# Gated MLP of a two-layer decoder trunk: the fourth chunk pair of each layer by seven half-size block products instead of two plain products, with the three plain pairs left in front of it issued in a new order

## The chip, the cores and the metric

The kernel runs on one core of one Trainium2 chip, as one launch. The metric is the device time of one execution in microseconds (us). The kernel before takes 1432.87 us, the median of three runs (1432.86 to 1433.24).

## The reference, cut to what matters

```python
def conv_ffn(x, norm, w_up, dw_w, dw_b, w_down):      # D_MODEL 1024, D_FF 3072, SEQ 512, float32
    h = rms_norm(x, norm) @ w_up
    g = causal_dwconv(h[..., :D_FF], dw_w, dw_b)      # width 3
    u = h[..., D_FF:]
    return (jax.nn.gelu(g) * u) @ w_down
```

Both layers end with this block, after a mixer and a cross-attention; the change is in this block alone. Tokens lie along the free axis of every tile (512 of them), channels on the 128 partitions.

## The kernel before

**Precision.** TensorE multiplies `float32r` operands. Each float32 operand is kept as a high part (a copy by ScalarE, ACT) and a low part (the rest, by VectorE, DVE), and each product is three matmuls: high by high, high by low, low by high (`mm3`, L184 to L187). So every weight that is loaded costs a high on ACT and a low on DVE before TensorE (PE) can use it.

**Chunks.** `w_up` has 24 gate chunks and 24 value chunks of 128 columns; gate chunk c and value chunk c make pair c. In each layer `opening` computes pairs 0 to 3 plainly: `start(i)` is one chunk, eight contraction tiles by three matmuls of 512 columns, so 24 matmuls a chunk and 48 a pair. Pairs 4 to 23 go through `unit(c)`: gate and value chunk, the two halves of the contraction and the two halves of the tokens make a two by two block product, which is done with seven products of 4 by 3 matmuls of 256 columns, 84 matmuls in all. Their operands are sums: on the token side T1 to T4, made once per layer by `Seven.sums`; on the weight side the blocks a11, a12, a22, s1, s2, s3, s4. A block is `high(name)` on ACT, then `low(name)` on DVE.

**How the weight sums are made.** `Blocks` holds a pair's four quarter blocks: r and z (one load, `load`, L768), a12 and a22 (two loads, `load_second`, L773 and L774). After the low of a11 an accumulating DMA issued by GpSimd (POOL) adds z to r (L803), which makes s3; after the low of a22 one adds a22 to z (L805), which makes s1; after the low of s3 one adds a22 to r (L807), which makes s2; after the low of s2 one adds a12 to r (L811), which makes s4. So s2 of a pair cannot be copied before s3's low is done and a 256 KB transfer has landed.

**A unit's order.** PE does B11 (a11), B21 (a12), T2 (s2), T3 (s3), then in a unit with a down projection one 12-matmul product of 512 columns (`Down.out`, into an `aux` bank), then T1 (s1), B22 (s4), T4 (a22), and a second `Down.out`. DVE and ACT meanwhile make the blocks of the next pair, add the seven results up (L170), and run `gating` of the pair before: scale by r (the norm's reciprocal, 512 wide), taps (two instructions, L857), Gelu on ACT, product (L861), high `ys[c][0]` (L863) and low `ys[c][1]` (L865). The first `Down.out` of group g needs ys of the four pairs 4g to 4g+3, the last of which was begun in the unit before.

**What sets the order.** PE, ACT, DVE and POOL run in the order in which the code of `opening` and `unit` is written (`manual_schedule` over `ORDERED`). The order of the loads on SyncE's queue (SP) is set by the tile framework's scheduler; each waits there for its buffer: a `raw` buffer (three of them) is free when the low of its last holder is done, a `big` buffer (fifteen) when its last reader is done.

**Names.** `first` and `second` are the first two pairs of `pairs`; `gate(i)`, `values(i)`, `close(i)` are the plain pair's gate branch, product and low of ys; `fetch(i)` loads a plain chunk's weights and makes their high, `w[-1].low()` their low; `rest()` is the end of the last plain pair, done inside the first unit.

Of the kernel before, what the change touches and what calls it, by code (L numbers as in the profile page):

```python
# [15 lines left out]
P = 128  # L16
# [8 lines left out]
CF = D_FF // P  # L25
NG = 6
GC = CF // NG
EPS = 1e-6
AHEAD = 100
PAIRED = (0, 4, 1, 5, 2, 6, 3, 7)  # L30
# [30 lines left out]
def trunk(ctx: ExitStack, tc: tile.TileContext, I: dict, out: list):  # L61
# [751 lines left out]
    def ffn(layer, norm, nxt, seven):  # L813
# [23 lines left out]
        downs = {c: Down(*divmod(c - GC, GC)) for c in range(GC, CF + GC)}  # L837

        def high(c, name):
            if c in pairs:  # L840
                pairs[c].high(name)

        def low(c, name):
            if c in pairs:
                pairs[c].low(name)

        def gating(c, f, g, ps, u3):
# [19 lines left out]
        def unit(c):  # L867
# [19 lines left out]
            ps = m(seven.B21, "a12")  # L887
# [5 lines left out]
            ps = m(seven.T2, "s2")  # L893
# [6 lines left out]
            ps = m(seven.T3, "s3")  # L900
# [11 lines left out]
            if c + 1 in downs:  # L912
# [25 lines left out]
        def opening():  # L938


            nonlocal left, due
            norm.r, ps, y = None, {}, [None] * GC

            def start(i):

                ps[i] = main_ps()
                x = w.pop(0)
                for k in range(C):
                    mm3(ps[i], blk(x, k * P), norm.x[k], k == 0, k == C - 1)

            def fetch(i):
                w.append(Piece(I["wup"][(layer * 2 + i % 2) * GC + i // 2]))
                w[-1].high()

            def gate(c):
# [15 lines left out]
            def values(c):  # L971
                V.tensor_tensor(y[c], ps.pop(2 * c + 1), y[c], op=ALU.mult)
                ys[c] = act_r(), act_r()
                A.activation(ys[c][0], y[c], AF.Copy)

            def close(c):
                V.tensor_tensor(ys[c][1], y[c], ys[c][0].bitcast(F32), op=ALU.subtract)
# [22 lines left out]
            next(g, None)  # L1000

# [36 lines left out]
            pairs[second].load()  # L1038
            pairs[second].load_second()
            downs[first].load()  # L1040
            values(2)
            close(2)
            high(second, "a11")

            start(7)
            downs[first].w.high()
            g = gate(3)
            next(g)
            low(second, "a11")
            next(g)  # L1050
            downs[first].w.low()
            next(g)
            downs[second].load()
            pairs[second + 1].load()
            next(g, None)

            def rest():
                values(3)
                yield
                close(3)  # L1060

            left, due = rest(), None

        left, due = None, None
        first, second = GC, GC + 1
        with tc.high_priority(AHEAD):
            w = [Piece(I["wup"][(layer * 2 + k) * GC]) for k in range(2)]
            for x in w:
                x.high()
                x.low()  # L1070
# [707 lines left out]
def _fours(g, v):  # L1778

    return np.concatenate([g[:, :, :T], v[:, :, :T], v[:, :, T:], g[:, :, T:]], axis=2)  # L1780


def _layout(inputs):
# [5 lines left out]
    for name, width in _PARAMS:  # L1789
# [25 lines left out]
        "wup": np.concatenate([_cols(w[:, at : at + GC * P]) for w in up for at in (0, CF * P)]),  # L1815
        "wpair": np.concatenate([_fours(w[GC:CF], w[CF + GC :]) for w in map(_cols, up)]),
# [22 lines left out]
```

## Time and profile before

| | |
|---|---|
| median of three runs | 1432.87 us |
| profiled execution, its own time | 1434.17 us |
| its span (first to last instruction) | 1432.3 us |
| PE busy | 1419.6 us, 99% of the span |
| DVE busy | 1176.7 us, 82% |
| ACT busy | 798.2 us, 56% |
| POOL busy | 304.4 us, 21% |
| granted TensorE clock | 0.999 |
| the MLP of layer 0 | from about 356 to 716 us of the span |
| the MLP of layer 1 | from about 1044 us on |

The profile is that of one execution, so a sum made from its rows is set against its own 1434.17 us, 1.3 us above the median. The busy share of an engine is an average over stages. PE's matmuls are pipelined: a row's duration is longer than the distance to the next start, and it is the distance that fills the time. In a timeline row the first number is the start in us from the span's start, the second the duration, and what stands in square brackets is the idle time of the engine before the row and what ended it.

### The profile page before, as it was taken

How to read it: one execution, taken by the hardware profiler on the slowest of the kernel's cores; microseconds unless marked ns; L12 is line 12 of the kernel's file. 1: busy time of each engine (PE TensorE's matmuls, PEld its weight loads, DVE VectorE, ACT ScalarE, POOL GpSimd, SP SyncE). 2: the span in 40 equal slices, each digit the busy share in tenths (PEclk: the TensorE clock that was granted, in tenths of full speed). 3: DMA queues.
4: the chain of work that ended last, by engine and by line, in shares of the span. 5: the costliest groups of instructions: out<-in, count | busy, mean ns of one | idle time of the engine just before them, and what ended most of it. 6: DMA issues, size and time to landing. Idle time of an engine off the chain costs nothing.

```text
span 1432.3 us, 22644 instructions
## 1 busy us (share of the span) xinstructions
PE 1419.6 (99%) x8504; PEld 1257.3 (88%) x8504; DVE 1176.7 (82%) x1955; ACT 798.2 (56%) x1321; POOL 304.4 (21%) x317
## 2 busy tenths in 40 slices
PE   9999999999999999999999999999999999999997
PEld 7888888998899999999988777899889999999997
DVE  6987776778788888888888997978778888888885
ACT  7678754666544444544565547767655444444434
POOL 0001310200021221222008992010001222222201
PEclk9999999999999999999999999999999999999999
DMA  8523232542557777777432464345244876787741
GB/s 292 198 81 99 93 118 81 118 111 89 158 136 169 162 182 165 163 173 173 136 123 89 118 167 143 107 87 147 87 129 121 178 179 157 171 184 159 162 126 59
DMA packets 77517, 200.11 MB, mean 140 GB/s; under 512 B 8672, under 2 KB 9952, under 8 KB 77408
## 3 DMA queue, kind: packets, MB, share of 16 engines
q1 hardware_dynamic: 50624, 150.15, 33.6%
q0 software_dynamic: 26496, 48.25, 20.5%
q8 instruction: 67, 1.10, 0.3%
q14 instruction: 42, 0.34, 0.1%
q10 hardware_dynamic: 288, 0.27, 0.1%
HBM read 145.16 MB, written 2.10 MB: 103 GB/s over the span
## 4 chain that ended last, share of the span: by engine, by line
PE 91%; DVE 3%; POOL 2%; DMA 2%; ACT 1%; issue 1%; SPq 0%; POOLq 0%; ACTq 0%; DVEq 0%
PE mm L186 22%; PE mm L185 22%; PE mm L187 22%; PE aux L185 7%; PE aux L186 7%; PE aux L187 7%; PE mm L456 2%; DMA raw<-in_wv 1%; DVE wlo L166 1%; POOL actf L1443 1%; PE aux L529 0%; ACT whi L165 0%; POOL act L166 0%; POOL tmp L1264 0%; DMA raw<-in_win 0%
## 5 line engine op out<-in xcount | busy, mean ns | idle before, releaser
L186 PE MATMUL mm<-act,whi 128*128 128x512 f32 (+2 forms) x1093 | 385.1, 352 | 0.6 <-DVE act L180 0.5
L185 PE MATMUL mm<-act,whi 128*128 128x512 f32 (+2 forms) x1093 | 384.6, 353 | 0.1
L187 PE MATMUL mm<-act,wlo 128*128 128x512 f32 (+2 forms) x1093 | 384.6, 352 | 0.0
L186 PEld LDWEIGHTS mm<-act,whi 128*128 128x128 f32 x1093 | 206.6, 189 | 30.3 <-DVE act L166 1.0
L185 PEld LDWEIGHTS mm<-act,whi 128*128 128x128 f32 x1093 | 206.4, 189 | 30.0 <-ACT tmp L1442 0.8
L187 PEld LDWEIGHTS mm<-act,wlo 128*128 128x128 f32 x1093 | 206.6, 189 | 27.0
L793 ACT ACTIVATE bigr<-raw 128x512 fp32r<-128x512 f32 x160 | 100.7, 630 | 156.7 <-DMA raw<-wa 64.3
L187 PE MATMUL mm<-bigr,bigr 128*128 128x256 f32 x640 | 181.1, 283 | 0.0
L186 PE MATMUL mm<-bigr,bigr 128*128 128x256 f32 x640 | 181.1, 283 | 0.0
L185 PE MATMUL mm<-bigr,bigr 128*128 128x256 f32 x640 | 180.9, 283 | 0.0
L170 DVE TENSOR_TENSOR tmp<-mm,tmp 128x256 f32<-128x256 f32 x322 | 131.2, 420 | 34.7 <-PE mm L187 28.3
L185 PE MATMUL aux<-act,whi 128*128 128x512 f32 x399 | 156.3, 392 | 0.0
L186 PE MATMUL aux<-act,whi 128*128 128x512 f32 x399 | 156.2, 391 | 0.0
L187 PE MATMUL aux<-act,wlo 128*128 128x512 f32 x399 | 155.2, 389 | 0.0
L165 ACT ACTIVATE whi<-raw 128x1024 fp32r<-128x1024 f32 (+1 forms) x95 | 96.6, 1021 | 85.5 <-PE mm L186 44.5
L800 DVE TENSOR_TENSOR bigr<-raw,bigr 128x512 fp32r<-128x512 f32 x160 | 110.0, 688 | 32.4 <-ACT bigr L793 30.4
L186 PEld LDWEIGHTS mm<-bigr,bigr 128*128 128x128 f32 x640 | 122.7, 192 | 1.6
L185 PEld LDWEIGHTS mm<-bigr,bigr 128*128 128x128 f32 x640 | 122.7, 192 | 1.6
L187 PEld LDWEIGHTS mm<-bigr,bigr 128*128 128x128 f32 x640 | 122.7, 192 | 0.0
L803 POOL DMA_DIRECT2D raw<-raw x46 | 39.8, 866 | 350.8 <-DVE wlo L800 303.9
L166 DVE TENSOR_TENSOR wlo<-raw,whi 128x1024 fp32r<-128x1024 f32 (+1 forms) x75 | 90.7, 1212 | 19.7 <-ACT whi L165 19.5
L807 POOL DMA_DIRECT2D raw<-wa x46 | 39.7, 864 | 303.2 <-DVE bigr L800 253.6
(341 smaller groups left out, 3013.4 us busy)
## 6 DMA issues: line engine op xcount, KB each, us to landing
raw<-wa POOLq DMA_DIRECT2D x138, 256.0 KB, 4.4
big<-in_wdown SPq DMA_DIRECT2D x42, 512.0 KB, 6.7
wa<-in_wpair SPq DMA_DIRECT2D x80, 256.0 KB, 3.4
raw<-in_wpair SPq DMA_DIRECT2D x40, 512.0 KB, 5.7
raw<-in_pw SPq DMA_DIRECT2D x24, 512.0 KB, 3.5
raw<-raw POOLq DMA_DIRECT2D x46, 256.0 KB, 7.3
raw<-in_win SPq DMA_DIRECT2D x20, 512.0 KB, 3.4
raw<-in_wk SPq DMA_DIRECT2D x16, 512.0 KB, 3.7
```

The lines of the kernel that those rows point to most:

```text
L165: A.activation(hi, src, AF.Copy)
L166: fetched[1] = (eng or V).tensor_tensor(lo, src, hi.bitcast(F32), op=ALU.subtract)
L170: V.tensor_tensor(out, a, b, op=ALU.add)
L185: PE.matmul(ps, wh, xh, start=first, stop=False)
L186: PE.matmul(ps, wh, xl, start=False, stop=False)
L187: PE.matmul(ps, wl, xh, start=False, stop=last)
L456: PE.matmul(p, m[j], x, start=k == 0 and j == 0 and x is hi, stop=k == C - 1 and x is lo)
L793: A.activation(self.w[name][0], self.block(name), AF.Copy)
L800: V.tensor_tensor(lo, self.block(name), hi.bitcast(F32), op=ALU.subtract)
L803: G.dma_start(self.r, self.z, accum_op=ALU.add)
L807: G.dma_start(self.r, self.a22, accum_op=ALU.add)
L1443: G.tensor_tensor(z[:, s:], z[:, s:], f[:, s:], op=ALU.add)
```

## The change

Pair 3 leaves `opening` and becomes the first `unit`, in both layers. `opening` then has six plain chunks, `start(0)` to `start(5)`, in place of eight, and `first` and `second` are pairs 3 and 4. The new `unit(3)` has no down projection in it: the first one needs ys of pairs 0 to 3 and stands in `unit(4)`, as before. So that `unit(3)` has less to make, the blocks a11, a22 and a12 of pair 4 are made in `opening` already (`early`), and so is the low of the first `w_down` piece. What `opening` issues is written in another order throughout.

The core of the diff:

```diff
-        pairs = {c: Blocks(I["wpair"][layer * (CF - GC) + c - GC]) for c in range(GC, CF)}
+        pairs = {c: Blocks(I["wpair"][layer * (CF - PLAIN) + c - PLAIN]) for c in range(PLAIN, CF)}   # PLAIN = 3
...
-            if c + 1 in downs:
+            if c >= GC and c + 1 in downs:
                 downs[c + 1].w.high()
...
             start(1)
             fetch(3)
-            w[-1].low()
+            high(first, "s3")
             g = gate(0)
             next(g)
-            high(first, "s3")
             high(first, "s1")
+            w[-1].low()
+            next(g)
             next(g)
             low(first, "s3")
-            next(g)
             low(first, "s1")
             next(g, None)
...
             start(3)
             fetch(5)
-            w[-1].low()
+            downs[GC].load()
+            pairs[second].load_second()
+            high(first, "s2")
             g = gate(1)
             next(g)
-            high(first, "s2")
+            w[-1].low()
+            pairs[second].load()
+            next(g)
+            t = seven.sums(3)
+            next(t)
             next(g)
             low(first, "s2")
-            next(g)
+            next(t, None)
             next(g, None)

             start(4)
-            fetch(6)
-            w[-1].low()
+            high(second, "a11")
             values(1)
-            t = seven.sums(3)
-            next(t)
+            low(second, "a11")
+            early.add((second, "a11"))
             close(1)
-            next(t, None)

             start(5)
-            fetch(7)
-            w[-1].low()
+            downs[GC].w.high()
             g = gate(2)
             next(g)
+            high(second, "a22")
+            downs[GC].w.low()
             next(g)
             next(g)
+            high(second, "a12")
+            low(second, "a22")
             next(g, None)
-
-            start(6)
...
-            start(7)
...
+            low(second, "a12")
+            early.update(((second, "a22"), (second, "a12")))
             pairs[second + 1].load()
-            next(g, None)
...
-        first, second = GC, GC + 1
+        first, second = PLAIN, PLAIN + 1
...
-            for c in range(GC, CF):
+            for c in range(PLAIN, CF):
                 unit(c)
```

The rest of the diff follows from it: `early` keeps `unit` from making a block twice, `rest()` ends pair 2 in place of pair 3, and the host lays out three plain pairs and twenty-one block pairs per layer.

How it moves instructions, at three places in layer 0. On ACT, in `start(1)`, from the high of the fourth plain chunk (L199, now L200) to the first Gelu; raw_3530 holds r and z of the first block pair. Before, then of the change:

```order
L199 ACTIVATE whi_3618<-raw_3616 128x1024
L960 ACTIVATE tmp_3624<-tmp_3622,par 128x512
L793 ACTIVATE bigr_3626<-raw_3530 128x512
L793 ACTIVATE bigr_3628<-raw_3530 128x512
L967 ACT_TABLE_LOAD
L967 ACTIVATE tmp_3624<-tmp_3624 128x512
```

```order
L200 ACTIVATE whi_3618<-raw_3616 128x1024
L794 ACTIVATE bigr_3621<-raw_3530 128x512
L963 ACTIVATE tmp_3625<-tmp_3623,par 128x512
L794 ACTIVATE bigr_3627<-raw_3530 128x512
L970 ACT_TABLE_LOAD
L970 ACTIVATE tmp_3625<-tmp_3625 128x512
```

The high of s3 now stands ahead of the scaling by the middle tap (L963); the high of s1 still stands ahead of the table load and the Gelu.

On SP, the loads of the MLP of layer 0 from the fourth plain chunk on, up to the second `w_down` piece of the change. Before, then of the change:

```order
L194 DMA raw_3616<-in_wup 128x1024
L194 DMA raw_3662<-in_wup 128x1024
L194 DMA raw_3698<-in_wup 128x1024
L773 DMA wa_3994<-in_wpair 128x512
L194 DMA raw_3741<-in_wup 128x1024
L194 DMA raw_3795<-in_wup 128x1024
L194 DMA big_3840<-in_wdown 128x1024
L194 DMA big_3888<-in_wdown 128x1024
L768 DMA raw_3834<-in_wpair 128x1024
```

```order
L195 DMA raw_3616<-in_wup 128x1024
L195 DMA raw_3662<-in_wup 128x1024
L195 DMA big_3703<-in_wdown 128x1024
L195 DMA raw_3698<-in_wup 128x1024
L774 DMA wa_3901<-in_wpair 128x512
L769 DMA raw_3716<-in_wpair 128x1024
L769 DMA raw_3820<-in_wpair 128x1024
L775 DMA wa_3902<-in_wpair 128x512
L195 DMA big_3905<-in_wdown 128x1024
```

The first `w_down` piece (big_3703) now stands right behind the fifth plain chunk (raw_3662), four loads earlier than big_3840 did; the loads of the seventh and eighth plain chunks are gone.

On DVE, from the last plain pair's low of ys (L977, now L980) on, where the first unit's work begins: before in `unit(4)`, then of the change in `unit(3)`; L170 and L171 are the additions of the products.

```order
L977 TENSOR_TENSOR act_3912<-tmp_3880,act_3911 128x512
L800 TENSOR_TENSOR bigr_3915<-raw_3834,bigr_3915 128x512
L800 TENSOR_TENSOR bigr_3917<-wa_3837,bigr_3917 128x512
L170 TENSOR_TENSOR tmp_3894<-mm_3920,tmp_3895 128x256
L170 TENSOR_TENSOR tmp_3895<-mm_3938,tmp_3895 128x256
L800 TENSOR_TENSOR bigr_3951<-raw_3530,bigr_3951 128x512
L800 TENSOR_TENSOR wlo_3954<-raw_3890,whi_3953 128x512
L800 TENSOR_TENSOR wlo_3848<-wa_3836,whi_3847 128x512
L170 TENSOR_TENSOR tmp_3896<-mm_3959,tmp_3895 128x256
L202 TENSOR_TENSOR wlo_3990<-big_3888,whi_3989 128x1024
L832 TENSOR_TENSOR x<-x,aux_3976 128x512
```

```order
L980 TENSOR_TENSOR act_3841<-tmp_3807,act_3840 128x512
L801 TENSOR_TENSOR bigr_3844<-raw_3716,bigr_3844 128x512
L171 TENSOR_TENSOR tmp_3823<-mm_3847,tmp_3824 128x256
L171 TENSOR_TENSOR tmp_3824<-mm_3863,tmp_3824 128x256
L801 TENSOR_TENSOR bigr_3876<-raw_3530,bigr_3876 128x512
L801 TENSOR_TENSOR wlo_3879<-raw_3820,whi_3878 128x512
L171 TENSOR_TENSOR tmp_3825<-mm_3883,tmp_3824 128x256
L171 TENSOR_TENSOR tmp_3825<-mm_3907,tmp_3824 128x256
L171 TENSOR_TENSOR tmp_3822<-mm_3907,tmp_3825 128x256
L801 TENSOR_TENSOR bigr_3920<-raw_3716,bigr_3920 128x512
L171 TENSOR_TENSOR tmp_3823<-mm_3924,tmp_3825 128x256
```

The lows of a22 and a12 of the next pair, the low of a `w_down` piece and the addition into x are gone from here; the low of s3 (bigr_3844) is second in both, the low of s4 of the running pair (bigr_3876) fifth in place of sixth, and and between the low of s3 and that of s2 (bigr_3920) stand seven instructions in place of eleven.

More of the change, by code (lines that the diff above doesn't have):

```diff
@@ L27 @@
 GC = CF // NG
+PLAIN = 3
 EPS = 1e-6
@@ L834, in sum @@
                     nxt.feed(n)
-        pairs = {c: Blocks(I["wpair"][layer * (CF - GC) + c - GC]) for c in range(GC, CF)}
+        pairs = {c: Blocks(I["wpair"][layer * (CF - PLAIN) + c - PLAIN]) for c in range(PLAIN, CF)}
         downs = {c: Down(*divmod(c - GC, GC)) for c in range(GC, CF + GC)}
+        early = set()
         def high(c, name):
-            if c in pairs:
+            if c in pairs and (c, name) not in early:
                 pairs[c].high(name)
         def low(c, name):
-            if c in pairs:
+            if c in pairs and (c, name) not in early:
                 pairs[c].low(name)
@@ L911, in unit @@
                 pairs[c + 2].load_second()
-            if c + 1 in downs:
+            if c >= GC and c + 1 in downs:
                 downs[c + 1].w.low()
@@ L941, in opening @@
             nonlocal left, due
-            norm.r, ps, y = None, {}, [None] * GC
+            norm.r, ps, y = None, {}, [None] * PLAIN
             def start(i):
@@ L1009, in opening @@
             fetch(5)
-            w[-1].low()
+            downs[GC].load()
+            pairs[second].load_second()
+            high(first, "s2")
             g = gate(1)
             next(g)
-            high(first, "s2")
+            w[-1].low()
[3 more added lines that the diff above has]
+            next(t)
             next(g)
             low(first, "s2")
-            next(g)
+            next(t, None)
             next(g, None)
             start(4)
-            fetch(6)
-            w[-1].low()
+            high(second, "a11")
             values(1)
-            t = seven.sums(3)
-            next(t)
+            low(second, "a11")
+            early.add((second, "a11"))
             close(1)
-            next(t, None)
             start(5)
-            fetch(7)
-            w[-1].low()
+            downs[GC].w.high()
             g = gate(2)
             next(g)
+            high(second, "a22")
+            downs[GC].w.low()
             next(g)
             next(g)
+            high(second, "a12")
+            low(second, "a22")
             next(g, None)
-            start(6)
[L1038 to L1043, printed above, removed]
-            start(7)
[L1046 to L1053, printed above, removed]
+            low(second, "a12")
+            early.update(((second, "a22"), (second, "a12")))
             pairs[second + 1].load()
-            next(g, None)
             def rest():
-                values(3)
+                values(2)
                 yield
-                close(3)
+                close(2)
             left, due = rest(), None
         left, due = None, None
-        first, second = GC, GC + 1
+        first, second = PLAIN, PLAIN + 1
         with tc.high_priority(AHEAD):
-            w = [Piece(I["wup"][(layer * 2 + k) * GC]) for k in range(2)]
+            w = [Piece(I["wup"][(layer * 2 + k) * PLAIN]) for k in range(2)]
             for x in w:
```

6 lines of the change are left out of this document (3 added, 3 removed).

## The prediction

> **What bounds the kernel now.** I read the page first: share of the span by engine (part 1), then the chain that ended last (part 4).
>
> ```profile
> PE 1419.6 (99%) x8504; PEld 1257.3 (88%) x8504; DVE 1176.7 (82%) x1955; ACT 798.2 (56%) x1321; POOL 304.4 (21%) x317
> PE 91%; DVE 3%; POOL 2%; DMA 2%; ACT 1%; issue 1%; SPq 0%; POOLq 0%; ACTq 0%; DVEq 0%
> ```
>
> PE is the bound, and its stream of matmuls is the end of the chain nearly everywhere. Then the waits of PE, longest first, and the busy time by stretches of the MLP of layer 0 (PE, PEld, DVE, ACT, POOL, clock, DMA share):
>
> ```profile
> PE stat L297 <- DVE actf L1458: 1.8, 1, 1.8
> ...
> PE mm L186 <- DVE act L180: 0.5, 1, 0.5
> 330.00:400.00 70.00, 70.00 (x310) 57.96 (x309) 58.15 (x93) 43.92 (x70) 3.84 (x5) 1.00 0.44 128
> 416.00:431.00 15.00, 15.00 (x107) 14.06 (x106) 14.49 (x26) 7.07 (x12) 3.47 (x4) 1.00 0.76 179
> ```
>
> None of the listed waits lies in the MLP, and PE has no gap there, neither in `opening` nor in a unit. So only two things change the time: the PE time of the steps themselves, and waits that did not exist. DVE is close behind PE in a unit, at 14.49 of 15.00 us.
>
> **What is removed.** The timeline of PE gives the distance from one start to the next, for 512 and for 256 columns:
>
> ```profile
> 389.67 0.39 PE L187 MATMUL mm<-act,wlo 128*128 128x512 f32 x1
> ...
> 399.87 0.39 PE L187 MATMUL mm<-act,wlo 128*128 128x512 f32 x1
> ...
> 400.21 0.28 PE L186 MATMUL mm<-act,whi 128*128 128x256 f32 x1
> ...
> 405.61 0.28 PE L186 MATMUL mm<-bigr,bigr 128*128 128x256 f32 x1
> ```
>
> 45 steps take 10.20 us, so 0.2267 each, and 45 steps take 5.40 us, so 0.120 each. A plain pair is 48 × 0.2267 = 10.88 us, a block pair 84 × 0.120 = 10.08 us. The change saves 0.80 us in each layer, 1.6 us in all, and it can save no more, since PE has no wait there to lose. That is the lower end.
>
> By the Trainium skill ("TensorE: Matmul & The Clock Gate", section "Back-to-back issue gap"), the gap is N/2.4 + 2.5 ns: 215.8 and 109.2 ns. By it the saving would be 10.36 − 9.17 = 1.2 us a layer, 2.4 in all; the rows above differ, and they decide.
>
> **What is added beside PE.** Bytes from memory stay (two 512 KB pieces against one of 512 and two of 256 KB). POOL gets four more accumulating transfers a layer. DVE loses a plain pair's two 1024-wide lows, four 512-wide instructions and two taps, and gets a unit's seven lows, seven 256-wide additions, four 512-wide instructions and two taps; at the spacings below that is 6.2 against 10.5 us, 4.3 us more. From 330 to 400 us DVE is free for 70.00 − 58.15 = 11.85 us, so it fits on average; the question is the order, and whether anything that PE needs comes late. The new `unit(3)` is only 10.08 us long, and its ys is wanted in the next unit after 5.76 us of products (4 × 1.44) instead of 5.76 + 2.72: the first `Down.out` is the due date to check.
>
> **When ys of pair 3 is ready.** I follow the chain from the last row that stands in the same place in both orders, the low of the first a11, in the clock of the trace before:
>
> ```profile
> 361.99 0.68 DVE L800 TENSOR_TENSOR wlo<-raw,whi 128x512 fp32r<-128x512 f32 x1
> 362.97 0.86 POOL L803 DMA_DIRECT2D raw<-raw x1 [70.52 <-DVE wlo L800]
> 367.43 0.86 POOL L805 DMA_DIRECT2D raw<-wa x1 [3.60 <-DMA raw<-raw]
> 370.25 1.27 ACT L793 ACTIVATE bigr<-raw 128x512 fp32r<-128x512 f32 x2
> 372.00 1.28 ACT L967 ACT_TABLE_LOAD   x1 [0.47 <-DVE tmp L963]
> 373.29 0.64 ACT L967 ACTIVATE tmp<-tmp 128x512 f32<-128x512 f32 x1
> 373.96 0.69 DVE L969 TENSOR_TENSOR tmp<-tmp,r 128x512 f32<-128x512 f32 x1 [0.84 <-ACT tmp L967]
> 375.36 1.22 DVE L202 TENSOR_TENSOR wlo<-raw,whi 128x1024 fp32r<-128x1024 f32 x1
> ```
>
> POOL issues z-to-r (L803) 0.3 us after that low; it lands after X. Then 0.3 to the issue of a22-to-z (L805), which lands after Y. The high of s1 starts 0.1 later and takes 0.62; the table load 1.28 and the Gelu 0.64 are queued behind it on ACT. So the Gelu ends at 362.97 + X + 0.3 + Y + 0.1 + 0.62 + 1.28 + 0.64 = 365.9 + X + Y. From there to the end of the fifth chunk's low it is as before, 376.58 − 373.93 = 2.65: 368.55 + X + Y.
>
> From there DVE works without a break to the low of s4 in `unit(3)`, 31 instructions in the change's order. Their spacing:
>
> ```profile
> 390.23 1.22 DVE L202 TENSOR_TENSOR wlo<-raw,whi 128x1024 fp32r<-128x1024 f32 x1
> 391.36 0.69 DVE L957 TENSOR_TENSOR tmp<-mm,r 128x512 f32<-128x512 f32 x1
> 392.94 1.54 DVE L963 SCALAR_TENSOR_TENSOR tmp<-tmp,par,tmp 128x511 f32<-128x511 f32 x2 [0.89 <-ACT tmp L960]
> 397.43 0.69 DVE L977 TENSOR_TENSOR act<-tmp,act 128x512 fp32r<-128x512 f32 x1 [0.70 <-ACT act L974]
> ...
> 418.57 0.69 DVE L861 SCALAR_TENSOR_TENSOR tmp<-tmp,tmp 128x512 f32<-128x512 f32 x1 [0.16 <-ACT tmp L859]
> 419.36 0.69 DVE L800 TENSOR_TENSOR bigr<-raw,bigr 128x512 fp32r<-128x512 f32 x1
> 419.97 0.69 DVE L800 TENSOR_TENSOR bigr<-wa,bigr 128x512 fp32r<-128x512 f32 x1
> 420.57 0.42 DVE L170 TENSOR_TENSOR tmp<-mm,tmp 128x256 f32<-128x256 f32 x1
> 420.90 0.68 DVE L865 TENSOR_TENSOR act<-tmp,act 128x512 fp32r<-128x512 f32 x1
> ```
>
> Two 1024-wide lows at 1.13 (391.36 − 390.23), two pairs of taps at 1.45, ten 256-wide at 0.33, fourteen 512-wide at 0.61, and the low of s4 itself 0.69: 2.26 + 2.90 + 3.3 + 8.5 + 0.7 = 17.7. One trip to ACT and back, for the last plain pair's ys, adds 0.7 (the row at 397.43), and short waits for an instruction just ahead or a Gelu just in time about 1.1, an estimate from 0.16 (the row at 418.57) at some seven places. Together 19.5: the low of s4 ends at 388.05 + X + Y, that of s3, 1.3 earlier, at 386.7 + X + Y.
>
> Now the longest link. The second transfer that matters, a22-to-r (L807, which gives s2 of pair 4), is issued 0.3 later, at 387.0 + X + Y, and lands after Z. On DVE the low of s2 stands ahead of the additions of `unit(3)`'s last two products and of its whole gating, so all of that waits for it. What follows a landing is seen in `unit(4)` of the trace before, where L807 landed at 406.16 + 5.1:
>
> ```profile
> 411.34 0.63 ACT L793 ACTIVATE bigr<-raw 128x512 fp32r<-128x512 f32 x1 [3.16 <-DVE tmp L170]
> 414.61 0.69 DVE L800 TENSOR_TENSOR bigr<-raw,bigr 128x512 fp32r<-128x512 f32 x1 [0.85 <-ACT bigr L793]
> 419.75 0.62 ACT L863 ACTIVATE act<-tmp 128x512 fp32r<-128x512 f32 x1
> 742.86 0.50 PE L186 MATMUL mm<-act,whi 128*128 128x512 f32 x1 [0.53 <-DVE act L180]
> 743.20 0.40 PE L187 MATMUL mm<-act,wlo 128*128 128x512 f32 x1
> ```
>
> From the landing to the high of ys 420.37 − 411.26 = 9.1, less the 0.85 that DVE waited for s1 there (in the change a22 was summed long before): 8.3. The low of ys ends 1.2 after the high (421.58). So PE has ys at 387.0 + 8.3 + 1.2 = 396.5 + X + Y + Z.
>
> PE wants it: `unit(3)` starts when six chunks are done, 400.10 − 10.88 = 389.22; 10.08 for it, 5.76 for four products, nine matmuls and one more at 0.2267: 407.3. The cost in a layer is X + Y + Z − 10.8, and 0.1 for each of two restarts (0.34 in place of 0.23 at 742.86): X + Y + Z − 10.6, or nothing if that is below nothing.
>
> **The three transfers.** Time to landing, as the trace has it, in this order: L803 in this place; L803 in the same place of layer 1; L805 in this place; L811 at 382.4, with three loads of 512 KB in flight and a fourth issued while it runs; L807 of `unit(4)`, at 406.16 between loads issued at 406.04 and 407.76; L807 of `unit(5)`, with none in flight. The last row is the page's median of all L803.
>
> ```profile
> DMA to landing us min/median/max: 4.2/4.2/4.2
> DMA to landing us min/median/max: 3.7/3.7/3.7
> DMA to landing us min/median/max: 3.4/3.4/3.4
> DMA to landing us min/median/max: 6.0/6.0/6.0
> DMA to landing us min/median/max: 5.1/5.1/5.1
> DMA to landing us min/median/max: 3.3/3.3/3.3
> ...
> raw<-raw POOLq DMA_DIRECT2D x46, 256.0 KB, 7.3
> ```
>
> X: before, one load was in flight beside L803; now the first `w_down` piece stands right behind it on SP, two loads of 512 KB. Ends 3.7 and 6.0; I take 5.5, between the row with two loads (5.1) and that with three and more (6.0), since both are issued before it here. Y: 3.4 as now, up to 4.2 if the next load comes under it; 3.5. Z: 3.3 with nothing beside it, 5.1 with two loads; the second `w_down` piece goes out when the s2 product frees its buffer, some 2 us ahead, and a wpair load behind the low of s4, 1 us after it; 4.0. The sum is 13.0, the cost 2.4 us a layer, 4.8 in all. Net **4.8 − 1.6 = +3.2 us**: 1437.4 on the profiled execution's own 1434.17, and 1436.1 on the median, which I take as the base of every time here.
>
> One due date lies on the way: B22's low of s4 at 389.22 + 7.2 + 0.24 = 396.7, so X + Y up to 8.6; beyond, part of the same lateness shows there first. The fifth chunk's low is wanted by about 378.7: it stalls PE only from X + Y = 10.1. The other edits cost nothing: the earlier highs on ACT lie in its free 26 us of those 70, POOL is busy for 3.84, and without that cover each high would cost 0.62.
>
> **Rivals.** *All of it hidden*: if X + Y + Z is at most 10.6, ys is in time and the saving stands: −1.6, 1431.3. For it: 3.7 + 3.4 + 3.3 = 10.4 have all occurred. Against: no row with two loads in flight was under 5.1. *Equal turns*: POOL's queue shares with SP's queue as a whole, however many loads wait there, so X is that of one load all along, 4.5 (4.2, where the load was half done). Then 4.5 + 3.4 + 4.0 − 10.6 = 1.3 a layer, +1.0: 1433.9. The Trainium skill states such a rule ("DMA: Bandwidth & Descriptors", section "Queues, rings and completion order"): an engine takes turns between queues, a packet at a time. The 6.0 with three loads in flight speaks against it. *The opening itself late*: X + Y beyond 10.1, at the 7.3 that L803 has in the median; then the fifth chunk's low, s4 and ys are late one after the other. With X + Y = 11 and Z = 4.6 that is 5.0 a layer: +8.4, 1441.3. That a 256-wide step costs more in the new unit than 0.120 is excluded by the forty units that run.
>
> **How the numbers follow.** Late ys 0.55, its own range 1434.0 to 1438.5 (X + Y + Z from 12.0 to 14.2); hidden 0.12; equal turns 0.18; opening late 0.15. About 0.2%, 2.9 us, is what a measurement of this kernel can tell from no change: slower by more means over 1435.7, which is two thirds of the first (0.38) and all of the last, 0.53. Faster by more needs −2.9, beyond the whole saving: 0.01. The rest, 0.46, is within. The range takes in the lower end, 1431.2, and with the upper ends 6.0 + 4.2 + 5.1 = 15.3, 4.7 a layer, +7.8, 1440.5.
>
> **What will show it.** In the waits of PE two new ones a layer on an `aux` product, for the high and then the low of ys, 1 us each, perhaps one of some tenths for s4. POOL's z-to-r of the first block pair landing after 5 us or more. DVE without idle time from about 378 us until s2. PE's steps in `unit(3)` at 0.120. I am wrong if ys comes before 407, or if a wait of PE stands elsewhere.

## The result and the profile after

The changed kernel takes 1439.92 us, the median of six runs (1439.48 to 1441.91), against 1432.86 us for the kernel before (six runs, 1431.95 to 1433.42): the ratio is 1.0053 with a 95% interval from 1.0042 to 1.0063. The change makes the kernel 7.06 us slower, where 3.2 was forecast. The profiled execution of the changed kernel took 1441.91 us by itself, 7.74 us more than the 1434.17 of the profiled execution before.

PE is still the bound. From the page after, the engines and the chain that ended last:

```profile
PE 1421.2 (99%) x8576; PEld 1258.9 (87%) x8576; DVE 1185.2 (82%) x1979; ACT 800.2 (56%) x1333; POOL 310.8 (22%) x325
...
PE 83%; DVE 5%; DMA 4%; ACT 3%; issue 3%; POOL 2%; SPq 0%; POOLq 0%; ACTq 0%; DVEq 0%
```

The share of PE in the chain fell from 91% to 83%: the chain now leaves PE for some stretch. The waits of PE after say for what: the three numbers are us in total, how many times, and the longest (before, none of these rows was there; one of the three for `wlo` lies outside the MLP, at 34 us):

```profile
PE mm L188 <- DVE wlo L203: 2.2, 3, 1.0
PE mm L188 <- DVE bigr L801: 1.9, 2, 1.0
PE aux L187 <- DVE act L868: 1.4, 2, 0.7
...
PE aux L186 <- ACT act L866: 0.7, 2, 0.4
...
PE mm L186 <- ACT whi L200: 0.2, 1, 0.2
```

PE's timeline has their places in layer 0, and two rows of the new `unit(3)`, the first of B11 and one of T3, 45 steps apart:

```profile
380.13 0.50 PE L188 MATMUL mm<-act,wlo 128*128 128x512 f32 x1 [0.97 <-DVE wlo L203]
...
390.72 0.28 PE L186 MATMUL mm<-act,whi 128*128 128x256 f32 x1
...
396.11 0.28 PE L186 MATMUL mm<-bigr,bigr 128*128 128x256 f32 x1
...
399.40 0.39 PE L188 MATMUL mm<-act,bigr 128*128 128x256 f32 x1 [0.97 <-DVE bigr L801]
...
410.50 0.50 PE L186 MATMUL aux<-act,whi 128*128 128x512 f32 x1 [0.38 <-ACT act L866]
411.73 0.50 PE L187 MATMUL aux<-act,whi 128*128 128x512 f32 x1 [0.72 <-DVE act L868]
```

The steps between 390.72 and 396.11 are 0.120 us each, as in the other units. PE waits three times: at 380.13 for the low of the fifth plain chunk, at 399.40 for the low of s4 in `unit(3)`, and from 410 on for the high and the low of ys of pair 3. Layer 1 has the same three places (1071.70, 1090.97 and 1103.22). Why, the chain of waits of the stretch from 359 to 412 us shows; each row is a start, how long it held the chain, and what it was:

```profile
362.88 6.60 DMA raw<-raw
369.48 0.28 issue
369.76 5.07 DMA raw<-wa
...
375.50 1.28 ACT L970
376.79 0.64 ACT tmp L970
377.46 0.71 DVE tmp L972
...
378.86 0.81 DVE wlo L203
...
398.37 3.91 DMA raw<-wa
402.37 0.64 ACT bigr L794
...
411.07 0.61 DVE act L868
411.73 0.50 PE aux L187
```

From the low at 378.86 to the issue of a22-to-r at 398.37 this view goes by POOL (it puts a z-to-r of pair 4 there), but POOL's own row names DVE, whose low of s3 (bigr, 397.38) is what the prediction has there:

```profile
398.37 0.86 POOL L808 DMA_DIRECT2D raw<-wa  x1 [2.77 <-DVE bigr L801]
```

So it is the chain of the prediction: X = 6.60, Y = 5.07, Z = 3.91. In layer 1 the same three transfers took 6.2, 5.7 and 3.8 us to land:

```profile
DMA to landing us min/median/max: 6.2/6.2/6.2
...
DMA to landing us min/median/max: 5.7/5.7/5.7
...
DMA to landing us min/median/max: 3.8/3.8/3.8
```

SP's queue after, around the first two of them:

```profile
362.00 0.33 SPq L195 DMA_DIRECT2D raw<-in_wup  x1
362.38 0.42 SPq L195 DMA_DIRECT2D big<-in_wdown  x1
369.62 0.33 SPq L195 DMA_DIRECT2D raw<-in_wup  x1
```

z-to-r goes out at 362.88, 0.5 us behind the first `w_down` piece. Being 2.4 us later to land than before (6.6 for 4.2), it lets a22-to-z go out at 369.76, 0.14 us behind the load of the sixth chunk (369.62); before, a22-to-z was issued at 367.43, 1.4 us ahead of that load, and landed after 3.4. In layer 1 of after it goes out 0.23 us ahead of that load (1060.73 and 1060.96) and takes 5.7 all the same, so it need not be behind the load to be late: lying beside it is enough.

### The profile page after: what moved, and what is told of

Its sections match the earlier page's. It is cut to its first block, busy times and chain, and to the rows that moved or that the text cites. A ratio compares the mean times of both kernels' runs of the same rounds, so it can differ in the third digit from the quotient of the medians.

```text
span 1440.1 us, 22866 instructions
## 1 busy us (share of the span) xinstructions
PE 1421.2 (99%) x8576; PEld 1258.9 (87%) x8576; DVE 1185.2 (82%) x1979; ACT 800.2 (56%) x1333; POOL 310.8 (22%) x325
## 4 chain that ended last, share of the span: by engine, by line
PE 83%; DVE 5%; DMA 4%; ACT 3%; issue 3%; POOL 2%; SPq 0%; POOLq 0%; ACTq 0%; DVEq 0%
PE mm L188 20%; PE mm L187 20%; PE mm L186 20%; PE aux L187 7%; PE aux L186 7%; PE aux L188 7%; DMA raw<-raw 1%; PE mm L457 1%; DMA raw<-in_wv 1%; DMA raw<-wa 1%; DVE wlo L167 1%; POOL actf L1436 1%; ACT whi L166 1%; DMA raw<-in_wk 0%; PE aux L530 0%
## 5 line engine op out<-in xcount | busy, mean ns | idle before, releaser
L188 PE MATMUL mm<-act,wlo 128*128 128x512 f32 (+2 forms) x1077 | 376.9, 350 | 1.9 <-DVE wlo L203 1.9
L187 PE MATMUL mm<-act,whi 128*128 128x512 f32 (+2 forms) x1077 | 377.2, 350 | 0.6 <-DVE act L181 0.5
L186 PE MATMUL mm<-act,whi 128*128 128x512 f32 (+2 forms) x1077 | 376.9, 351 | 0.4 <-ACT whi L200 0.2
L186 PEld LDWEIGHTS mm<-act,whi 128*128 128x128 f32 x1077 | 203.4, 189 | 29.9 <-ACT whi L200 1.1
L187 PEld LDWEIGHTS mm<-act,whi 128*128 128x128 f32 x1077 | 203.7, 189 | 29.0 <-DVE act L167 1.0
L188 PEld LDWEIGHTS mm<-act,wlo 128*128 128x128 f32 x1077 | 203.6, 189 | 28.4 <-DVE wlo L203 2.8
L794 ACT ACTIVATE bigr<-raw 128x512 fp32r<-128x512 f32 x168 | 105.2, 629 | 176.9 <-DMA raw<-wa 68.6
L188 PE MATMUL mm<-bigr,bigr 128*128 128x256 f32 x672 | 190.2, 283 | 0.0
L187 PE MATMUL mm<-bigr,bigr 128*128 128x256 f32 x672 | 190.1, 283 | 0.0
L186 PE MATMUL mm<-bigr,bigr 128*128 128x256 f32 x672 | 190.0, 283 | 0.0
L171 DVE TENSOR_TENSOR tmp<-mm,tmp 128x256 f32<-128x256 f32 x336 | 136.3, 419 | 34.4 <-PE mm L188 28.7
L801 DVE TENSOR_TENSOR bigr<-raw,bigr 128x512 fp32r<-128x512 f32 x168 | 115.5, 688 | 40.9 <-ACT bigr L794 38.6
L187 PEld LDWEIGHTS mm<-bigr,bigr 128*128 128x128 f32 x672 | 128.8, 192 | 1.6
L186 PEld LDWEIGHTS mm<-bigr,bigr 128*128 128x128 f32 x672 | 128.8, 192 | 1.6
L188 PEld LDWEIGHTS mm<-bigr,bigr 128*128 128x128 f32 x672 | 128.8, 192 | 0.0
```

Source lines behind the costliest of these rows:

```text
L171: V.tensor_tensor(out, a, b, op=ALU.add)
L186: PE.matmul(ps, wh, xh, start=first, stop=False)
L187: PE.matmul(ps, wh, xl, start=False, stop=False)
L188: PE.matmul(ps, wl, xh, start=False, stop=last)
L794: A.activation(self.w[name][0], self.block(name), AF.Copy)
L801: V.tensor_tensor(lo, self.block(name), hi.bitcast(F32), op=ALU.subtract)
```

## The experiments

The theory behind the prediction, called **loads** below: the two transfers of POOL last long because loads lie beside them, and their sum with Z, less the slack of 10.6 us, is the cost in a layer. Its rivals: **backlog** (the new order and the 4.3 us more of DVE work make DVE late, the loads only show it), **long link** (only Z counts), and **equal turns** (the number of loads beside a transfer of POOL does not matter).

**Run e1: the first `w_down` piece behind the sixth chunk's load.**

```diff
             fetch(5)
-            downs[GC].load()
+            with tc.issue_after(fetched[0].ins):
+                downs[GC].load()
```

> The kernel after, with one edit: on SP the first w_down piece of each layer is issued behind the load of the sixth plain chunk in place of ahead of it; nothing else moves. Theory 'loads': the piece beside z-to-r made X 6.6 in place of 4.2 us, and the late a22-to-z, issued behind the sixth chunk's load, made Y 5.1 in place of 3.4. Then X is 4.2 to 4.5 and Y 3.4 to 3.6 here, the waits of PE for the fifth chunk's low (1.1 us) and for the low of s4 (1.1 us) go in both layers. ys then depends on the last link: a22-to-r is issued some 3.5 us earlier, beside the second w_down piece, so Z is between the 3.9 seen and the 6.0 that a transfer with three loads beside it took; the cost is 7.8 + Z - 10.6, so 1.1 to 3.5 us a layer, all of it in the two waits for ys: 1433.5 to 1438.3, most likely 1436. Theory 'backlog' (DVE's and ACT's own order and 4.3 us more of DVE work make it late, the loads only show it): the first wait goes, but s4 and ys stay as late as they are, 1438 to 1440. Theory 'long link' (only Z matters): no change, 1440.

Measured: 1442.21 us (four runs, 1440.35 to 1443.89; ratio to the kernel before 1.0062, 1.0047 to 1.0077). So it is not faster, and all three theories missed the time. The transfers in layer 0, z-to-r, a22-to-z, a22-to-r; then SP and POOL around the last; then PE's waits:

```profile
DMA to landing us min/median/max: 4.1/4.1/4.1
...
DMA to landing us min/median/max: 3.2/3.2/3.2
...
DMA to landing us min/median/max: 6.8/6.8/6.8
```

```profile
392.57 0.33 SPq L195 DMA_DIRECT2D big<-in_wdown  x1
393.96 0.33 SPq L769 DMA_DIRECT2D raw<-in_wpair  x1
```

```profile
392.96 0.86 POOL L808 DMA_DIRECT2D raw<-wa  x1 [2.51 <-DVE bigr L801]
```

```profile
PE aux L186 <- ACT act L866: 3.5, 2, 1.8
PE aux L187 <- DVE act L868: 1.4, 2, 0.7
```

X and Y came out as "loads" had them, and with them the waits for the fifth chunk's low and for s4 went in both layers: so the piece made those, and "long link" falls. But a22-to-r, now issued 31.2 us behind z-to-r in place of 35.5, falls 0.4 us behind the second `w_down` piece and 1.0 us ahead of a wpair load, and took 6.8 us (7.5 in layer 1) in place of 3.9. The sum is 14.1 and 14.8, so 3.5 and 4.2 us a layer, 1431.3 + 7.7 = 1439.0, with nearly all of it at ys (in layer 1 0.2 us stand a little ahead, at T2 of `unit(4)`, which wants the s2 that a22-to-r makes). The rest is a thing not foreseen, in the windows of layer 0 (the figure before the last two is the granted clock of PE):

```profile
410.00:414.00 4.00, 4.00 (x23) 4.00 (x22) 4.00 (x9) 1.07 (x2) 0.86 (x1) 0.57 0.99 225
414.00:420.00 6.00, 6.00 (x42) 5.50 (x40) 5.47 (x11) 2.02 (x4) 0.86 (x1) 1.00 0.69 137
```

Behind the two waits for ys PE ran at about half its clock from 410.4 to 413.7 us: its 256-wide steps took 0.213 us in place of 0.120, 16 of them, so 1.5 us more. The same stands behind the waits for ys of layer 1, at 1103, and at about 741 us, behind a wait of 1.15 us for the next norm's sum. Three of them make 4.5 us, so 1443.5; that execution took 1443.7 by itself.

**Run e2: the kernel before, with the piece early.**

```diff
             fetch(4)
+            downs[first].load()
+            early = fetched[0].ins
...
-            fetch(5)
+            with tc.issue_after(early):
+                fetch(5)
...
-            downs[first].load()
```

> The kernel before, with the first w_down piece of each layer issued directly behind the load of the fifth plain chunk, where the change put it; the order on PE, ACT, DVE and POOL stays that of before. Theory 'loads': z-to-r takes 6 to 6.6 us in place of 4.2 and a22-to-z about 5 in place of 3.4, so the low of the fifth plain chunk ends at about 376.6 + 4 = 380.6 in place of 376.6, where PE wants it by 378.7: a wait of about 1.1 us in each layer for that low, and no other, since DVE has 11.85 us free in 330 to 400 there: 1432.9 + 2.3 = about 1435, with 1434 to 1436. Theory 'backlog': without the new order nothing is late, 1432.9. Theory 'equal turns' (POOL's queue shares with SP's queue as a whole, however many loads wait there): z-to-r takes 4.5 at most, no wait, 1432.9.

Measured: 1437.10 us (ten runs, 1435.26 to 1438.02; ratio 1.0028, 1.0019 to 1.0037), against 1432.53 for the kernel before beside it. The sign and the mechanism are those of "loads", the size is twice that forecast. The profiled execution is the fastest of the ten (1435.26). In its layer 1 z-to-r and a22-to-z took

```profile
DMA to landing us min/median/max: 6.4/6.4/6.4
...
DMA to landing us min/median/max: 5.6/5.6/5.6
```

and PE waits for the high and the low of the fifth chunk:

```profile
1065.46 0.50 PE L185 MATMUL mm<-act,whi 128*128 128x512 f32 x1 [0.34 <-ACT whi L199]
...
1067.17 0.50 PE L187 MATMUL mm<-act,wlo 128*128 128x512 f32 x1 [0.98 <-DVE wlo L202]
```

In layer 0 they took 6.1 and 4.3, 10.4 in sum, and PE was held by some 0.2 us only (a start 0.44 us behind the one before, in place of 0.23; no wait is listed). So the place of one load, without the new order and without the new unit, makes the first of the three waits: "backlog" and "equal turns" both gave nothing here, and fall. What the slower nine executions spent up to 2.8 us more on is not in a profile. X and Y differ from layer to layer by as much; and the mean granted clock is 0.999 in the three shortest executions and 0.997 or 0.998 in six of the other seven, so slow stretches as in e1 may have part in it. That is not shown.

**Run e9: half the gating ahead of s2.**

```diff
             ps = m(seven.B22, "s4")
-            low(c + 1, "s2")
+            if c > PLAIN:
+                low(c + 1, "s2")
...
             next(left)
+            if c == PLAIN:
+                low(c + 1, "s2")
             low(c + 1, "s1")
```

> The kernel after, with one edit: in the first unit (pair 3) DVE's low of s2 of the next pair stands behind the addition of the B22 product and the scaling by r, not ahead of them, so that half of the gating no longer waits for Z. Theory 'loads': X and Y stay 6.6 and 5.1, the waits for the fifth chunk's low and the low of s4 (1.1 us each) stay in both layers, the wait for ys shrinks from 1.4 us to some tenths or to nothing at most: 0.5 to 1.4 us a layer, 1437 to 1439. Theory 'long link' (Z in front of the gating is what costs): all of it goes, down to 1433 or less. Theory 'backlog': as 'loads' or less, 1439 to 1440.

Measured: 1438.90 us (five runs, 1436.28 to 1440.55; ratio 1.0041, 1.0027 to 1.0056). As "loads" said, but for one layer: in the profile the waits for s4 stay at 1.0 us in both layers, that for ys falls to 0.3 (low alone), and the fifth chunk's low is waited for in layer 1, where X + Y is 6.8 + 4.7 = 11.5, and not in layer 0, where it is 5.7 + 4.2 = 9.9: on either side of the 10.1 of the prediction. "Long link" wanted 1433 or less and falls again; the time alone does not tell "loads" from "backlog" here.

**Run e10: loads moved and the gating ahead.** Besides the edit of e1, the second piece goes behind the wpair load of pair 6, and in `unit(3)` the low of s2 behind the first scaling, as in e9, and that of s1 behind the taps (the expectation says the taps of both; it holds for s1).

```diff
-            if c + 2 in downs and c + 2 <= CF:
+            if c + 2 in downs and c + 2 <= CF and c > PLAIN:
                 downs[c + 2].load()
...
+            if c == PLAIN:
+                with tc.issue_after(pairs[c + 3].fetched.ins):
+                    downs[c + 2].load()
             left = gating(c, f, g, ps, u3)
             next(left)
+            if c == PLAIN:
+                low(c + 1, "s2")
+                next(left)
+                low(c + 1, "s1")
+                return
```

> The kernel after with all links shortened: the first w_down piece behind the sixth chunk's load, the second w_down piece (for the unit of pair 5) behind the wpair load of pair 6, and in the first unit the additions, both scalings and the taps of the gating ahead of the lows of s2 and s1 on DVE. Theory 'loads' with the sum X + Y + Z - 10.6: X 4.2 to 4.5, Y 3.4 to 3.6, and Z no longer ahead of the gating, so ys is ready before PE wants it and no wait of PE is left in the first units; the saving of 1.6 us against before stands whole: 1431.3, with 1430.5 to 1432.5. Theory 'backlog': DVE's order in opening still makes s4 and ys late by 1 us or more a layer: 1434 or more. If a block-pair unit costs more than 84 x 0.120 us here, the time stays above before's without any wait.

Measured: 1431.91 us (ten runs, 1430.71 to 1432.71; ratio to before 0.9993, 0.9984 to 1.0003). No wait of PE is left in the first units. Its longest waits on what DVE makes all lie outside the MLP:

```profile
PE stat L298 <- DVE actf L1461: 0.8, 1, 0.8
PE stat L314 <- DVE tmp L248: 0.7, 1, 0.7
PE mm L187 <- DVE act L181: 0.5, 1, 0.5
```

The second, at 735 us, behind the MLP of layer 0, is not among the waits before: PE comes to the sum of the next norm earlier than DVE has its input, and part of the 1.6 us goes there. So 8.0 us of difference between after and this run lie in loads and in the place of two lows, none in the number of instructions.

**Run e4: both loads moved, no order of an engine changed.**

```diff
-            downs[GC].load()
+            with tc.issue_after(fetched[0].ins):
+                downs[GC].load()
...
+            if c == PLAIN:
+                with tc.issue_after(pairs[c + 3].fetched.ins):
+                    downs[c + 2].load()
```

> The kernel after with both w_down loads moved on SP: the first piece behind the sixth chunk's load (as in the run e1), and the second, which e1's z-to-r of pair 4... more exactly a22-to-r of pair 4 met 0.4 us after its issue, behind the wpair load of pair 6. All engine orders as in after. Theory 'loads, three terms': X 4.1, Y 3.2 as in e1, and Z back from 6.8 to 3.9 or less, since the second piece is no longer beside it; cost 11.2 - 10.6 = 0.6 us a layer: 1431.3 + 1.2 = 1432.5, up to 1434.5 if the wait for the low of ys (0.7 to 1.0) stays whole. No stretch at half the clock, since no wait is as long as e1's 2.5 us. Theory 'backlog': the ys waits stay at e1's 2.5 us a layer, 1439 or more.

Measured: 1432.16 us (ten runs, 1431.23 to 1433.90; ratio 0.9995, 0.9985 to 1.0004). The three transfers in layer 0:

```profile
DMA to landing us min/median/max: 4.2/4.2/4.2
...
DMA to landing us min/median/max: 3.2/3.2/3.2
...
DMA to landing us min/median/max: 3.9/3.9/3.9
```

The sum is 11.3, and no wait of the first units is in the list of PE's waits; by its starts PE is held 0.3 us there, at the low of ys, where the formula X + Y + Z − 10.6 gives 0.7. With the engine orders of after untouched, the place of two loads alone takes back 7.8 us. "Backlog" has nothing left to explain, and e1's 6.8 us was the second piece.

**Run e5: two pieces beside z-to-r.**

```diff
             fetch(4)
+            downs[GC].load()
+            downs[GC + 1].load()
...
             fetch(5)
-            downs[GC].load()
```

> The kernel after with the second w_down piece also issued directly behind the first, so that two of them (512 KB each) wait behind the fifth chunk's load when z-to-r is issued; its later load in the first unit goes. Theory 'share by queue' (SP's queue as a whole takes a share, however many loads wait in it, and takes it as long as anything waits there): X as in after, 6 to 6.8 us, Y 4 to 6, Z 3.3 to 3.9: 1437 to 1440. Theory 'share by load' (every load in flight takes its own share): the one piece took X from 4.1 to 6.5, a second takes it to 8.5 or more, the fifth chunk's low is 2 us later still: about 1444 or more, with PE waits of 3 us for that low.

Measured: 1439.90 us (four runs, 1438.52 to 1441.40; ratio 1.0051, 1.0036 to 1.0066). The time is what "share by queue" gave, the transfers are not: z-to-r took 5.7 us in layer 0 and 8.3 in layer 1, a22-to-z 4.1 and 3.3. In layer 0 SP needed 2.59 us to issue the two pieces, in layer 1 1.15, so the pieces may not have lain beside z-to-r in the same way. It stays open how the chip divides the engines between the two queues; that one piece more need not cost more time is shown, since the sums X + Y, 9.8 and 11.6, are not above after's 11.7 and 11.9.

**Run e3: s1 behind the Gelu.**

```diff
-            high(first, "s1")
             w[-1].low()
             next(g)
             next(g)
+            high(first, "s1")
             low(first, "s3")
```

> The kernel after with one edit: ACT's high of s1 stands behind the table load and the first Gelu, not ahead, so that Y no longer delays the Gelu; loads as in after. Theory 'loads': X stays 6 to 6.8 and Y 4 to 5.7; the Gelu ends about 3 us earlier, the waits for the fifth chunk's low and the low of s4 go or are some tenths, and ys is late by what is left, 2 to 2.5 us a layer in one place: 1435.5 on the waits alone; if a wait of 2.5 us also costs a stretch at half the clock, as in e1 (1.5 us a layer), 1438.5. Theory 'X alone' (the high of s3 in front of the middle tap holds the Gelu, not s1): no change, 1440.

Measured: 1437.71 us (seven runs, 1434.31 to 1439.38; ratio 1.0033, 1.0022 to 1.0044). The loads were not as in after, which the expectation took for granted: with this edit on ACT the framework's scheduler issued the first `w_down` piece behind the sixth chunk's load, X fell to 4.1, and the run tells of e1's state, not of s1. Z was 5.3, the waits for ys in layer 0 were 1.39 and 0.72, and PE again ran at half its clock behind them.

**Run e6: the same, with the load held in its place.**

```diff
-            fetch(5)
             downs[GC].load()
+            with tc.issue_after(fetched[0].ins):
+                fetch(5)
```

> The edit of the run e3 again (ACT's high of s1 behind the table load and the first Gelu), now with the first w_down piece kept directly behind the fifth chunk's load as in after, which e3 had lost: there the edit on ACT had also moved that load behind the sixth chunk's. Theory 'loads': X 6 to 6.8, Y 4 to 5.7 as in after. The Gelu no longer waits for s1, but DVE's low of s1, which stands ahead of the product behind the Gelu, still does: in after it starts at 375.51 and ends at 376.2, and the product starts at 377.46, so DVE gains 1.25 us and no more. The wait for the fifth chunk's low (1.1 us) goes in both layers, the waits for the low of s4 and for ys stay: 1439.9 - 2.5 = 1437.4, with 1436.5 to 1438.5. Theory 'X alone' (the high of s3 holds the Gelu): no change, 1440. Theory 'backlog' (DVE's own work): no change in any of the three waits.

Measured: 1438.45 us (five runs, 1437.18 to 1438.51; ratio 1.0037, 1.0023 to 1.0051). X was 6.0 and 6.3, Y 5.8 and 5.7. PE's waits in layer 0 and the first of layer 1:

```profile
396.30 0.39 PE L188 MATMUL mm<-act,bigr 128*128 128x256 f32 x1 [0.97 <-DVE bigr L801]
...
407.40 0.50 PE L186 MATMUL aux<-act,whi 128*128 128x512 f32 x1 [0.37 <-ACT act L866]
408.63 0.50 PE L187 MATMUL aux<-act,whi 128*128 128x512 f32 x1 [0.72 <-DVE act L868]
...
1068.02 0.50 PE L188 MATMUL mm<-act,wlo 128*128 128x512 f32 x1 [0.25 <-DVE wlo L203]
```

The wait for the fifth chunk's low is gone (0.25 is left in layer 1), the other two stand as in after: the chain of the prediction through ACT's order, high of s1 ahead of the Gelu, is shown, and it carries that one wait. The gain, 1.5 us, is less than the 2.5 forecast.

**Run e13: a wait made on purpose.** On the kernel of e10:

```diff
-            add(f[:, :M], ps, u3)
+            for _ in range(8 if c == PLAIN else 1):
+                add(f[:, :M], ps, u3)
```

> The kernel of run e10 (no PE wait in the first units, 1431.9) with seven needless repeats of one 256-wide DVE addition in the gating of the first unit, 0.45 us each, so that PE waits for ys as long as in e1, about 2.5 us a layer in two pieces 1.2 us apart, and for no other reason. Theory 'clock' (a wait of this length is followed by about 3 us at half the clock, which cost e1 1.5 us a layer): 1431.9 + 2 x (2.5 + 1.5) = 1439.9, with granted clock near 0.5 in about 3 us behind the wait. Theory 'wait only' (e1's slow stretches were chance): 1431.9 + 5.0 = 1436.9, and clock 1.0 there.

Measured: 1437.05 us (six runs, 1436.39 to 1439.08; ratio 1.0031, 1.0018 to 1.0044). The waits came out shorter than aimed at; in layer 0, and then the clock in the windows behind them:

```profile
407.64 0.51 PE L186 MATMUL aux<-act,whi 128*128 128x512 f32 x1 [0.85 <-ACT act L867]
408.86 0.50 PE L187 MATMUL aux<-act,whi 128*128 128x512 f32 x1 [0.72 <-DVE act L869]
```

```profile
410.00:413.00 3.00, 3.00 (x16) 3.00 (x15) 3.00 (x6) 0.73 (x2) 0.86 (x1) 0.50 0.98 201
413.00:420.00 7.00, 7.00 (x48) 6.51 (x47) 5.97 (x12) 1.78 (x3) 0.86 (x1) 0.97 0.70 155
```

Both layers have the slow stretch in this execution, the longest of the six (1439.08). So it does not take the loads of e1: a wait that nothing but DVE's repeats makes can be followed by it too. It does not come in every execution, as it seems: the mean granted clock is 0.996 in the two longest (1439.08 and 1438.76) and 0.998 or 0.999 in the four from 1436.39 to 1437.37. Only the longest was profiled.

**Run e7: a shorter wait on purpose** (`range(5 ...)` in the line above).

> The kernel of run e13 with four repeats of the addition in place of seven, 1.36 us less, so that the waits of PE for ys in the first units are about 0.4 and 0.9 us a layer, as in after. Theory 'clock' (slow stretches come behind waits that together make up some half of about 3 us, and by where a window falls): none or few here, all executions near 1431.9 + 2.7 = 1434.6. Theory 'any wait': 1434.6 + 1.35 for each stretch, so up to 1437.3, as often as in run e13.

Measured: 1434.63 us (ten runs, 1432.80 to 1436.07; ratio 1.0014, 1.0005 to 1.0024). The profiled execution, the shortest, has one wait of 0.47 us a layer and no slow stretch. The median is where "clock" put it, but the spread of 3.3 us is not explained by that, so this run decides nothing.

**Run e8: the kernel of e10 again**, for a narrower interval.

> The kernel of run e10 again, in five rounds, to settle whether it beats the kernel before (there 1431.91 against 1432.53, ratio 0.9993 with 0.9984 to 1.0003). If the 1.6 us that the matmul steps save arrive whole, the ratio is 0.9989; if the wait of 0.7 us that its profile shows behind the MLP of layer 0 (on the next norm's sum) takes part of it in every execution, 0.9994; a ratio of 1 would mean that the saving is lost elsewhere.

Measured: 1431.92 us (eleven runs, 1430.58 to 1433.95) against 1432.69; ratio 0.9995, 0.9986 to 1.0004. It beats the changed kernel by 8 us; that it beats the kernel before is not shown, though the whole saving (0.9989) lies within the interval.

## Why the prediction was right in kind and short in size

- **What bounds, and the saving.** Right: PE bounds, its steps in `unit(3)` are 0.120 us, and without the new waits (e4, e10) the time is at or a little under that before. Of the 1.6 us, 0.6 to 0.8 were measured, with intervals that hold both 1.6 and nothing.
- **The chain.** Right in each link, by its own formulas and after's X, Y and Z in layer 0. The Gelu ends at 365.9 + 11.7 = 377.6 by the prediction and at 377.43 in the trace. The low of the fifth chunk follows by 380.3 and 380.08, a22-to-r is issued by 398.7 and at 398.37, the low of ys ends by 412.1 and at 411.68. So the estimate of 19.5 us for 31 instructions of DVE and the 8.3 and 1.2 us behind Z hold to 0.4 us.
- **X: the term that failed first.** 5.5 was taken, from rows with two and three loads beside a transfer of this kind, with 6.0 as upper end; 6.6 and 6.2 were measured here, 5.7 to 6.8 in e2, e9 and e6. The bound was only the largest of a few rows.
- **Y: the term that failed most.** 3.5 was taken, 4.2 at most; 5.1 and 5.7 were measured. The step that failed is "3.4 as now": Y was priced at its old place ahead of the sixth chunk's load, though X itself moves it. X's delay of 2.4 us puts the issue of a22-to-z right beside that load's. The prediction saw the case ("if the next load comes under it") but gave it 4.2 at most. Over all runs, Y was 4.1 to 5.8 in the nine cases in which a22-to-z was issued within 0.8 us of that load, on either side of it (after, e2, e5, e6, e9); it was 3.2 to 3.4 where it was issued 1.4 us or more ahead (before, e1, e4, e10), and 3.3 where it came 1.8 us behind (e5, layer 1). What sets it between 4.1 and 5.8 stays open.
- **Z.** Right: 4.0 was taken, 3.9 and 3.8 measured. But it is not a constant: in e1, with the chain earlier, it met the second piece and took 6.8 and 7.5.
- **Which rival came.** The prediction's "opening itself late", given 0.15: X + Y passed 10.1 and the fifth chunk's low, s4 and ys are late one after the other. Its formula gives 5.0 and 5.1 us a layer for after's rows, so +8.5; the profiled executions differ by 7.7, the medians by 7.1.
- **The formula, and luck.** By PE's starts the cost in layer 0 is 4.6 us and not 5.0: the same product (T1 of `unit(4)`) starts at 408.60 before and at 412.30 after, whose clock is 0.09 ahead, so 3.8 later, and 0.8 were saved. In e4 it is 0.3 for 0.7. So the formula is some 0.4 too dear in a layer. After's sums, 15.6 and 15.7, lie above the 15.3 that the range took in (whose +7.8 is 1440.7 on 1432.87, not 1440.5); that the time lies inside the range all the same, and only just, is luck: the dear formula makes up for the short X and Y.
- **The chances.** "Equal turns" (4.5 for X) fell with e2. The chance of 0.55 stood on Y alone: with X as measured, a Y up to 3.5 would have kept X + Y at 10.1.
- **Signs.** Those for the two waits on ys (0.4 and 0.7 us, where 1 us each was said) and for z-to-r landing after 5 us or more came; the sign for being wrong, a PE wait elsewhere, came too.

## What to carry to other kernels

When a transfer is late, its followers can meet other traffic: price each link of a chain at the time at which it will be issued, not at the time at which the old trace shows it, and do so again after a fix, since e1's repair of the first links only sent the last one into the next load. Where a scheduler places loads, look at the queue's order after every edit, even one on another engine (e3), and hold a load with an explicit order where its place matters. A wait of PE of a microsecond or two, in pieces, can cost more than itself.

## What the runs showed of the hardware

- **The clock of PE after short waits.** Waits of 1.76 and 0.73 us (e1), 1.39 and 0.72 (e3, layer 0), and 0.85 and 0.72 (e13), with one 512-wide matmul between the two, were followed within 2 us by a stretch of some 3.3 us at half the clock (a window of 3 us at 0.50 in e13), 1.5 us of loss; so was a single wait of 1.15 us (e1, at 740 us). The waits of after, 0.38 and 0.72, were not, and neither were 1.15 and 0.72 in layer 1 of e3, so length alone does not decide. The Trainium skill ("TensorE: Matmul & The Clock Gate", section "HAM oscillation — how this bites in real kernels") states the rule as no idle gaps of PE above about 3.4 us. The traces differ: the longest gap ahead of such a stretch here is 1.76 us, about half of that.
- **A transfer of POOL beside loads of SP.** The same 256 KB accumulation (z-to-r) took 3.7 to 4.2 us with one 512 KB load issued 0.9 us ahead of it (e1, e4, before) and 5.7 to 6.8 with a second issued 0.5 us ahead (after, e2, e6, e9). One load alone can do as much when it is issued at the same time: a22-to-z took 4.1 to 5.8 within 0.8 us of a load, 3.2 to 3.4 farther from it. The second of the loads varies in its issue: SP spent 0.42 us on it in after and 1.46 in layer 0 of e9, where X was the shorter of the two layers, 5.7.
